# Third attention: two heads' logits as 64-row products on the two halves of the array

## The chip, the cores and the metric

One NeuronCore of one Trainium2 chip runs the whole program. The metric is the device time of one execution in microseconds (us); here the median of three runs.

## The reference, cut to what matters

Two transformer blocks in float32 over 512 tokens of width 1024. The third of its three attentions, the one that changes, has 16 query heads on 4 key heads of width 64, all keys visible:

```python
q = apply_rope_2(rmsnorm(q.reshape(B, T, N_HEADS, HEAD_DIM), q_g), cos, sin)
k = apply_rope_2(rmsnorm(k.reshape(B, T, N_KV_HEADS, HEAD_DIM), k_g), cos, sin)
def one_block(q_blk):
    s = jnp.einsum('bqkgd,bskd->bkgqs', q_blk, k).astype(jnp.float32) * scale
    p = jax.nn.softmax(s, axis=-1).astype(v.dtype)
    return jnp.einsum('bkgqs,bskd->bqkgd', p, v)
```

## The kernel before

Activations lie with features on the 128 partitions and tokens along the free dimension. Every float32 operand of a matmul is split into a high part (rounded to `float32r`) and a low part (the rest), and a product becomes high x high + high x low + low x high (`mul3`).

The program isn't issued as it is written. `Sched.record` notes every operation with its operands; `Sched.order` then simulates the five engines with the prices of `Sched.cost` and emits each engine's queue in the order so found: at each free moment the operation that was recorded first among those ready, unless `later` moved it back. `gate` adds a predecessor. A tile is given a buffer at its first write, in the order of recording, so a missing buffer stops the operations that write to it. PSUM has eight banks: each of the tags `mm`, `lg`, `tp`, `po` has one for itself, four are shared, and `bank` limits what a tag may hold at once.

Layer c is the third attention. For each of its eight pairs of heads, `layer_c` projects q (`fm`, tag `mm`), applies `rope`, and calls `stacks`: tile `a` holds the high part of head 0 on rows 0 to 63 and its low part on rows 64 to 127, tile `b` the same of head 1 the other way round. `doubles` has prepared each key head as `kdh` (high part on both halves) and `kdl` (low part on both halves). So a head's logits for 128 queries are two matmuls over all 128 rows and 512 key columns: stack x `kdh` and stack x `kdl`. `heads` then works head by head: `softmax` makes the logits of four query blocks in `lg` banks, DVE masks them into `pr` with the row's minimum in `mn` (one custom instruction), ACT takes the exponential in place; `turned` transposes `pr` on PE into a `tp` bank and splits it into `th` and `tl`; two products per key block with `v` gather in a `po` bank. `pr` has three buffers, a head needs one. A reciprocal of the row sums follows for both heads together (`late`), then the split into `o`, from which `attn_out` computes the output projection, tile `st` in the profile.

All instructions carry line 423 of the profile, the emitting line; tiles tell them apart.

Of the kernel before, what the change touches and what calls it, by code (L numbers as in the profile page):

```python
# [11 lines left out]
F32 = mybir.dt.float32  # L12
F32R = mybir.dt.float32r
AF = mybir.ActivationFunctionType
ALU = mybir.AluOpType
# [3 lines left out]
P = 128  # L19
S = 512  # L20
# [3 lines left out]
NB = S // P  # L24
# [4 lines left out]
LARGE = 3.0e38  # L29
# [126 lines left out]
class Sched:  # L156
# [92 lines left out]
    @staticmethod  # L249
    def cost(o, outs, ins):  # L250

        ps = any(x.tile.pool.space is not None for x in ins)
        if o.name == "dma_start":
            x = (outs + ins)[0]
            late = 1550 + (x.box[1] - x.box[0]) * x.size * 4 / 360

            return (600, late + 2000) if o.eng == "gpsimd" else (60, late)
        n = max(x.size for x in outs + ins) if o.name in ("tensor_reduce", "bn_stats", "bn_aggr", "max") else outs[0].size
        if o.eng == "tensor":
            x = outs[0].size  # L260
            if o.name == "matmul" and ins[0].tile.dt == F32:
                return max(64, 4 * 0.42 * x), 200
            return max(107 if o.name == "transpose" else 54, 0.417 * x + 2.5), 200
        if o.eng == "scalar":
            aps = sum(isinstance(o.kw.get(k), View) for k in ("bias", "scale", "accum_out"))
            return (51 if ps else 93) + 0.834 * n + 93 * max(0, aps - 1) + (60 if aps == 1 else 0), 130
        if o.eng == "gpsimd":
            if o.name == "tensor_scalar":
                return 160 if n < 16 else 244 + 0.834 * n, 130
            if o.name == "memset":  # L270
                return 100, 130
            return (300 + 164 * n if n < 16 else 100 + 2.2 * n), 130
        c = 68 + 1.042 * n
        if o.name == "scalar_tensor_tensor" and isinstance(o.args[2], View):
            c += 61
        if o.name == "tensor_scalar" and not ps:
            c = 130 + 0.52 * n
        if o.name == "reciprocal":
            c = 70 + 6.3 * n
        return c, 130  # L280
# [219 lines left out]
class Net:  # L500
# [19 lines left out]
        return self.sched.tile(pool, tag, shape, dt, bufs, self.name(tag))  # L520

    def bank(self, tag):
        return self.t(self.pp, tag, [P, S], F32, {"mm": 3, "lg": 3, "tp": 3, "po": 2}[tag])

    def mm(self):
        return self.bank("mm")
# [240 lines left out]
    def softmax(self, pool, npr, lhs, rhs, W, masks, rows, sums, h, late):  # L767
# [20 lines left out]
                nc.gpsimd.tensor_scalar(p, p, rs, 1.0, ALU.mult, ALU.mult)  # L788
        return pr

    def inverses(self, pool, sums, n):

        nc = self.nc
        m = 2 * n
        rs = self.t(pool, "rs", [P, m])
        nc.vector.reciprocal(rs, sums)
        wide = self.t(pool, "top", [P, m * HD], bufs=1)
        nc.scalar.activation(wide.rearrange("p (a d) -> p a d", a=m), rs.rearrange("p (a o) -> p a o", o=1).to_broadcast([P, m, HD]), AF.Copy)
        ps = self.po()
        for b in range(n):  # L800
            nc.tensor.transpose(ps[:, b * P : (b + 1) * P], wide[:, b * P : (b + 1) * P], self.ident)
        return ps[:, : n * P]
# [16 lines left out]
        self.split(th[:, c], tl[:, c], tp[:, c])  # L819
        return th, tl, c  # L820

    def heads(self, pool, npr, nth, lhs, rhs, v, o, masks=None, causal=True, rows=(None, None), blocks=range(NB), narrow=False, late=False):


        nc = self.nc
        n = len(blocks) * P
        W = {i: (i + 1) * P if causal else S for i in blocks}
        keys = range(max(W.values()) // P)
        sums = self.t(pool, "sums", [P, 2 * len(blocks)])
        both = self.t(pool, "o", [P, n], bufs=1)  # L830
        for h in range(2):
            pr = self.softmax(pool, npr, lhs[h], rhs[h], W, masks, rows[h], sums, h, late)
            po = self.po()
            for b in keys:
                th, tl, c = self.turned(pool, nth, pr, W, b)
                if narrow:
                    for x, (part, y) in enumerate(((0, th), (0, tl), (64, th))):
                        nc.tensor.matmul(po[0:64, c], v[h][b][:, part : part + 64], y[:, c], start=b == 0 and x == 0, stop=b == keys[-1] and x == 2)
                else:
                    nc.tensor.matmul(po[:, c], v[h][b], th[:, c], start=b == 0, stop=False)  # L840
                    nc.tensor.matmul(po[:, c], v[h][b], tl[:, c], start=False, stop=b == keys[-1])
            r = slice(64 * h, 64 * h + 64)
            if narrow:
                nc.scalar.activation(both[r], po[0:64, :n], AF.Copy)
            else:
                top = self.t(pool, "top", [P, n], bufs=1)[0:64]
                nc.scalar.activation(top, po[0:64, :n], AF.Copy)
                nc.vector.tensor_tensor(both[r], po[64:128, :n], top, ALU.add)
        if late:
            nc.vector.tensor_tensor(both, self.inverses(pool, sums, len(blocks)), both, ALU.mult)  # L850
        self.split(o[0][:, :n], o[1][:, :n], both)
# [223 lines left out]
    def layer_c(self, x, gate, norm):  # L1075
        nc, I, tc = self.nc, self.I, self.tc
# [7 lines left out]
        with ExitStack() as c1:  # L1084
            pool = c1.enter_context(tc.tile_pool(name="c", bufs=2))
            tab = {}
            for w, col in (("q", V_QG), ("k", V_KG)):
                for m in range(2):
                    a = self.t(pool, f"tab{w}{m}", [P, S], bufs=1)
# [3 lines left out]
            v = [self.t(pool, f"v{b}", [P, 4, P], F32R, 1) for b in range(NB)]  # L1093
            bd = self.t(pool, "bd", [P, 2], bufs=1)
            zero = self.t(pool, "zero", [P, S], bufs=1)
# [5 lines left out]
            def inverse(ps, st):  # L1101

                sq = self.t(pool, "sqh", [P, S], bufs=1)
                nc.scalar.activation(sq, ps, AF.Square)
                for b in range(NB):
                    nc.tensor.matmul(st[:, 2 * b : 2 * b + 2], sq[:, b * P : (b + 1) * P], bd, start=True, stop=True)
                ms = self.t(pool, "msh", [P, 8])
                nc.vector.tensor_scalar(ms, st[:, 0:8], 1.0 / HD, EPS, ALU.mult, ALU.add)
                rr = self.t(pool, "rh", [P, 8], bufs=4)
                nc.gpsimd.tensor_tensor(rr, ms, self.mhalf, ALU.pow)  # L1110
                return rr
# [5 lines left out]
            kd = []  # L1117
            self.tm(I["w_v_c"], xh, xl, evac_v, ("po", "po", "lg", "tp"))
            for ps in kps:
                s = self.rope(pool, ps, tab["k", 0], tab["k", 1], nc.gpsimd)  # L1120
                st = self.lg()
                rr = inverse(ps, st)
# [6 lines left out]
            qs, o = [], []  # L1129
            for j in range(KD + 2):  # L1130
                if j < KD:
                    with self.sched.later(200 if j > 1 else 0):
                        self.low = nc.gpsimd if j > 2 else None
                        ps = q0 if j == 0 else self.fm(I["w_q_c"][j], xh, xl)
                        self.low = None
                        s = self.rope(pool, ps, tab["q", 0], tab["q", 1], nc.gpsimd if j else nc.vector)
                        rr = inverse(ps, ps)
                        qs.append((self.stacks(pool, "st", s, 16), rr))
                if j < 2:
                    continue  # L1140
                j -= 2
                st, rr = qs[j]
                n = j // 2
                o.append(self.two(pool, "st", 16))
                self.heads(pool, 3, 2, [(q, q) for q in st], [kd[n]] * 2, [[x[:, n, :] for x in v]] * 2, o[j], [zero] * NB, causal=False, late=True,
                           rows=[[rr[:, 2 * b + h : 2 * b + h + 1] for b in range(NB)] for h in range(2)])
            self.attn_out(o, I["w_o_c"], gate, norm)

# [314 lines left out]
```

## Time and profile before

| what | value |
|---|---|
| median of three runs | 2582.64 us (2580.6 to 2584.27) |
| profiled execution | 2581.65 us |
| its span, first to last instruction | 2579.8 us |
| PE busy | 2532.9 us, 98% |
| DVE busy | 1584.0 us, 61% |
| ACT busy | 1167.4 us, 45% |
| mean granted TensorE clock | 0.997 |

Busy times are shares of the whole span. PE is the matmul engine, PEld its weight loads, which run beside it; matmuls overlap in a pipeline, so the distance between two starts is the price of one, not its duration. DVE is the vector engine, ACT the scalar engine.

### The profile page before, as it was taken

The page shows a single profiled execution, that of the slowest core. Times are in us where ns is not written, and L with a number is a line of the kernel's source. Part 1 is how long each engine was busy: PE and PEld are TensorE (multiplying, and loading weights), DVE is VectorE, ACT ScalarE, POOL GpSimd, SP SyncE. Part 2 cuts the span into 40 slices and gives each one's busy share as a digit, 9 for nine tenths or more (in the row PEclk, how much of TensorE's full clock was granted, in tenths as well). Part 3 has the DMA queues.
Part 4 walks back from the last instruction along what each step waited for, and adds up shares of the span by engine and source line. Part 5 has one row for each costly group of instructions (what it writes and reads, how often), then busy time and mean ns, then how long its engine had stood idle before and what let it go on. Part 6 is the DMA issues. An engine that isn't in the chain of part 4 may idle for free.

```text
span 2579.8 us, 33446 instructions
## 1 busy us (share of the span) xinstructions
PE 2532.9 (98%) x12614; PEld 2124.3 (82%) x12614; DVE 1584.0 (61%) x2629; ACT 1167.4 (45%) x2104; POOL 404.3 (16%) x453
## 2 busy tenths in 40 slices
PE   8989999999999999999999999999999999999999
PEld 6779888888888888888877988888888888888887
DVE  7998666665488666666797534445447554634443
ACT  5677432334498422334786422333325444523322
POOL 4740100010162000013430200002002110200000
PEclk9999999999999999999999999999999999999999
DMA  4222655543222456542211233322333332333322
GB/s 154 86 70 83 198 188 169 189 139 108 90 72 93 142 186 189 166 159 94 83 37 44 92 98 98 99 93 96 106 106 115 99 95 86 97 98 98 98 97 91
DMA packets 90418, 290.47 MB, mean 113 GB/s; under 512 B 12400, under 2 KB 15728, under 8 KB 90256
## 3 DMA queue, kind: packets, MB, share of 16 engines
q1 hardware_dynamic: 75408, 237.80, 28.7%
q0 software_dynamic: 14848, 50.54, 6.5%
q8 instruction: 99, 1.62, 0.3%
q14 instruction: 63, 0.52, 0.1%
HBM read 277.28 MB, written 2.10 MB: 108 GB/s over the span
## 4 chain that ended last, share of the span: by engine, by line
PE 88%; DVE 7%; ACT 3%; issue 1%; DMA 1%; POOL 0%; SPq 0%; DVEq 0%; ACTq 0%; POOLq 0%
PE mm L423 76%; PE lg L423 4%; PE tp L423 4%; PE po L423 4%; DVE mask L423 1%; DVE st L423 1%; DVE acc L423 1%; DVE xl L423 0%; DVE pr L423 0%; ACT wh L423 0%; DVE o L423 0%; DVE y L423 0%; DVE m L423 0%; DVE wl L423 0%; ACT st L423 0%
## 5 line engine op out<-in xcount | busy, mean ns | idle before, releaser
L423 ACT ACTIVATE wh<-wr 128x1024 fp32r<-128x1024 f32 (+2 forms) x472 | 446.6, 952 | 1092.8 <-PE mm L423 946.0
L423 DVE TENSOR_TENSOR wl<-wr,wh 128x1024 fp32r<-128x1024 f32 (+1 forms) x374 | 449.5, 1202 | 307.6 <-ACT wh L423 298.8
L423 PE MATMUL mm<-xh,wh 128*128 128x512 f32 (+1 forms) x1640 | 625.2, 382 | 8.4 <-ACT wh L423 8.3
L423 PE MATMUL mm<-xl,wh 128*128 128x512 f32 (+1 forms) x1640 | 624.8, 381 | 0.6 <-POOL xl L423 0.4
L423 PE MATMUL mm<-xh,wl 128*128 128x512 f32 (+1 forms) x1640 | 624.9, 381 | 0.0
L423 PE MATMUL mm<-al,wh 128*128 128x512 f32 (+1 forms) x1072 | 407.1, 380 | 0.0
L423 PE MATMUL mm<-ah,wh 128*128 128x512 f32 (+1 forms) x1072 | 407.0, 380 | 0.0
L423 PE MATMUL mm<-ah,wl 128*128 128x512 f32 (+1 forms) x1072 | 406.8, 379 | 0.0
L423 PEld LDWEIGHTS mm<-xh,wh 128*128 128x128 f32 x1640 | 311.4, 190 | 62.6 <-ACT wh L423 9.0
L423 PEld LDWEIGHTS mm<-xl,wh 128*128 128x128 f32 x1640 | 311.9, 190 | 55.6 <-POOL xl L423 1.3
L423 PEld LDWEIGHTS mm<-xh,wl 128*128 128x128 f32 x1640 | 311.7, 190 | 55.0 <-DVE wl L423 0.8
L423 DVE SCALAR_TENSOR_TENSOR h<-mm,mod,h 128x512 f32<-128x512 f32 (+1 forms) x113 | 79.9, 707 | 261.5 <-PE mm L423 261.3
L423 PEld LDWEIGHTS mm<-al,wh 128*128 128x128 f32 x1072 | 201.6, 188 | 38.1
L423 PEld LDWEIGHTS mm<-ah,wh 128*128 128x128 f32 x1072 | 201.6, 188 | 38.1
L423 PEld LDWEIGHTS mm<-ah,wl 128*128 128x128 f32 x1072 | 201.6, 188 | 37.9
L423 POOL TENSOR_TENSOR wl<-wr,wh 128x512 fp32r<-128x512 f32 x98 | 133.1, 1369 | 219.5 <-ACT wh L423 214.7
L423 DVE TENSOR_TENSOR h<-mm,h 128x512 f32<-128x512 f32 (+1 forms) x91 | 56.5, 625 | 140.3 <-PE mm L423 140.3
L423 POOL DMA_DIRECT2D adaw<-in_ada_w x96 | 51.1, 533 | 532.6 <-DVE ada L423 469.5
L423 ACT ACTIVATE pr<-pr,mn 128x128 f32<-128x128 f32 (+2 forms) x192 | 116.6, 610 | 21.9 <-DVE mn L423 21.1
L423 ACT ACTIVATE ah<-a 128x512 fp32r<-128x512 f32 x128 | 81.0, 633 | 83.8 <-DVE a L423 81.7
L423 DVE SCALAR_TENSOR_TENSOR ada<-adaw,cs,ada 128x512 f32<-128x512 f32 x168 | 118.2, 745 | 0.0
L423 DVE TENSOR_TENSOR al<-a,ah 128x512 fp32r<-128x512 f32 x128 | 88.4, 692 | 42.0 <-ACT ah L423 41.9
(260 smaller groups left out, 3848.1 us busy)
## 6 DMA issues: line engine op xcount, KB each, us to landing
adaw<-in_ada_w POOLq DMA_DIRECT2D x96, 512.0 KB, 4.3
wr<-in_w_up SPq DMA_DIRECT2D x64, 512.0 KB
wr<-in_w_down SPq DMA_DIRECT2D x64, 512.0 KB
wr<-in_w_in SPq DMA_DIRECT2D x64, 512.0 KB
wr<-in_w_out SPq DMA_DIRECT2D x64, 512.0 KB
wr<-in_w_gu SPq DMA_DIRECT2D x24, 512.0 KB
wr<-in_w_gv SPq DMA_DIRECT2D x24, 512.0 KB
wr<-in_w_go SPq DMA_DIRECT2D x32, 384.0 KB
```

The costliest lines, as they stand in the source:

```text
L423: getattr(getattr(self.nc, o.eng), o.name)(*args, **kw)
```

## The change

For the third attention alone, a pair's q is only split into a high and a low tile of 128 rows (head 0 on rows 0 to 63, head 1 on rows 64 to 127). `pairs` computes the logits of both heads together: for each of high x high, high x low and low x high one matmul of 64 rows for head 0 and one for head 1, into two banks; all but the first of a group are gated on the second head's first. `softmaxes` masks and exponentiates both heads' blocks in turn, and `heads` transposes and multiplies them afterwards. `lg` may hold four banks in place of three, in the whole program. The planner prices a 64-row `float32r` matmul at half of its former price, at least 108 ns.

```diff
--- before.py
+++ after.py
@@ -260,7 +260,8 @@
             x = outs[0].size
             if o.name == "matmul" and ins[0].tile.dt == F32:
                 return max(64, 4 * 0.42 * x), 200
-            return max(107 if o.name == "transpose" else 54, 0.417 * x + 2.5), 200
+            c = max(107 if o.name == "transpose" else 54, 0.417 * x + 2.5)
+            return (max(108, c / 2) if ins[0].tile.dt == F32R and ins[0].box[1] - ins[0].box[0] == 64 else c), 200
         if o.eng == "scalar":
             aps = sum(isinstance(o.kw.get(k), View) for k in ("bias", "scale", "accum_out"))
             return (51 if ps else 93) + 0.834 * n + 93 * max(0, aps - 1) + (60 if aps == 1 else 0), 130
@@ -520,7 +521,7 @@
         return self.sched.tile(pool, tag, shape, dt, bufs, self.name(tag))
 
     def bank(self, tag):
-        return self.t(self.pp, tag, [P, S], F32, {"mm": 3, "lg": 3, "tp": 3, "po": 2}[tag])
+        return self.t(self.pp, tag, [P, S], F32, {"mm": 3, "lg": 4, "tp": 3, "po": 2}[tag])
 
     def mm(self):
         return self.bank("mm")
@@ -788,6 +789,35 @@
                 nc.gpsimd.tensor_scalar(p, p, rs, 1.0, ALU.mult, ALU.mult)
         return pr
 
+    def pairs(self, outs, q, k, tb, L):
+
+        nc, sched = self.nc, self.sched
+        n = len(sched.ops)
+        for j, (a, b) in enumerate(((q[0], k[0]), (q[0], k[1]), (q[1], k[0]))):
+            for h, ps in enumerate(outs):
+                r = slice(64 * h, 64 * h + 64)
+
+                sched.gate = n + 1 if j else None
+                nc.tensor.matmul(ps[:, :L], a[r, tb], b[r, :L], start=j == 0, stop=j == 2)
+        sched.gate = None
+
+    def softmaxes(self, pool, npr, q, k, W, masks, rows, sums):
+
+        nc = self.nc
+        prs = [self.t(pool, "pr", [P, sum(W.values())], bufs=npr) for _ in range(2)]
+        mns = [self.t(pool, "mn", [P, NB], bufs=4) for _ in range(2)]
+        f = 0
+        for n, (i, L) in enumerate(W.items()):
+            banks = [self.lg() for _ in range(2)]
+            self.pairs(banks, q, k, slice(i * P, (i + 1) * P), L)
+            x = slice(i, i + 1)
+            for h, (ps, pr, mn) in enumerate(zip(banks, prs, mns)):
+                p = pr[:, f : f + L]
+                nc.vector.tensor_tensor_reduce(p, ps[:, :L], masks[i][:, :L], 1.0 if rows[h] is None else rows[h][i], LARGE, ALU.add, ALU.min, mn[:, x])
+                nc.scalar.activation(p, p, AF.Exp, bias=mn[:, x], scale=-1.0, accum_out=sums[:, 2 * n + h : 2 * n + h + 1])
+            f += L
+        return prs
+
     def inverses(self, pool, sums, n):
 
         nc = self.nc
@@ -819,7 +849,8 @@
         self.split(th[:, c], tl[:, c], tp[:, c])
         return th, tl, c
 
-    def heads(self, pool, npr, nth, lhs, rhs, v, o, masks=None, causal=True, rows=(None, None), blocks=range(NB), narrow=False, late=False):
+    def heads(self, pool, npr, nth, lhs, rhs, v, o, masks=None, causal=True, rows=(None, None), blocks=range(NB), narrow=False, late=False, paired=None):
+
 
 
         nc = self.nc
@@ -828,8 +859,10 @@
         keys = range(max(W.values()) // P)
         sums = self.t(pool, "sums", [P, 2 * len(blocks)])
         both = self.t(pool, "o", [P, n], bufs=1)
+        if paired:
+            prs = self.softmaxes(pool, npr, *paired, W, masks, rows, sums)
         for h in range(2):
-            pr = self.softmax(pool, npr, lhs[h], rhs[h], W, masks, rows[h], sums, h, late)
+            pr = prs[h] if paired else self.softmax(pool, npr, lhs[h], rhs[h], W, masks, rows[h], sums, h, late)
             po = self.po()
             for b in keys:
                 th, tl, c = self.turned(pool, nth, pr, W, b)
@@ -1135,14 +1168,16 @@
                         self.low = None
                         s = self.rope(pool, ps, tab["q", 0], tab["q", 1], nc.gpsimd if j else nc.vector)
                         rr = inverse(ps, ps)
-                        qs.append((self.stacks(pool, "st", s, 16), rr))
+                        st = self.two(pool, "st", 16)
+                        self.split(*st, s)
+                        qs.append((st, rr))
                 if j < 2:
                     continue
                 j -= 2
                 st, rr = qs[j]
                 n = j // 2
                 o.append(self.two(pool, "st", 16))
-                self.heads(pool, 3, 2, [(q, q) for q in st], [kd[n]] * 2, [[x[:, n, :] for x in v]] * 2, o[j], [zero] * NB, causal=False, late=True,
+                self.heads(pool, 3, 2, None, None, [[x[:, n, :] for x in v]] * 2, o[j], [zero] * NB, causal=False, late=True, paired=(st, kd[n]),
                            rows=[[rr[:, 2 * b + h : 2 * b + h + 1] for b in range(NB)] for h in range(2)])
             self.attn_out(o, I["w_o_c"], gate, norm)
```

## Rows read from the trace of the kernel before

**Rows 1.** The page's head and first part: busy us, share of the span, instructions.
```profile
span 2579.8 us, 33446 instructions
PE 2532.9 (98%) x12614; PEld 2124.3 (82%) x12614; DVE 1584.0 (61%) x2629; ACT 1167.4 (45%) x2104; POOL 404.3 (16%) x453
```

**Rows 2.** The page's chain that ended last, by line.
```profile
PE mm L423 76%; PE lg L423 4%; PE tp L423 4%; PE po L423 4%; DVE mask L423 1%; DVE st L423 1%; DVE acc L423 1%; DVE xl L423 0%; DVE pr L423 0%; ACT wh L423 0%; DVE o L423 0%; DVE y L423 0%; DVE m L423 0%; DVE wl L423 0%; ACT st L423 0%
```

**Rows 3.** Windows of the third attention: length, engines' busy us, granted clock, DMA.
```profile
core 0: us, PE busy (x) PEld busy (x) DVE busy (x) ACT busy (x) POOL busy (x), PEclk, DMA share, GB/s
1253.40:1405.10 151.70, 147.38 (x797) 116.41 (x795) 133.94 (x273) 124.32 (x270) 39.56 (x28) 1.00 0.14 40
1270.00:1390.00 120.00, 118.82 (x649) 94.10 (x649) 111.75 (x228) 100.08 (x221) 34.89 (x25) 1.00 0.15 45
1404.00:1408.00 4.00, 2.87 (x9) 2.17 (x10) 2.12 (x4) 2.17 (x3) 0.00 (x0) 0.77 0.00 0
```

**Rows 4.** The chain that ended last from 1253.4 to 1405.1 us, by line.
```profile
by line: PE mm L423 28.0%; PE po L423 21.7%; PE tp L423 16.5%; PE lg L423 14.6%; DVE pr L423 3.8%; issue 3.0%; DVE o L423 2.7%; ACT kdh L423 1.7%; ACT pr L423 1.5%; DVE st L423 1.4%; ACT kdl L423 1.2%; ACT top L423 1.2%; ACT th L423 0.6%; D
```

**Rows 5.** Timeline of PE: start us, us, line, operation, count.
```profile
1290.66 0.39 PE L423 MATMUL lg<-kdh,st 128*128 128x512 f32 x1
...
1291.12 0.39 PE L423 MATMUL lg<-kdl,st 128*128 128x512 f32 x1
...
1300.93 0.39 PE L423 MATMUL lg<-kdl,st 128*128 128x512 f32 x1
1301.16 0.40 PE L423 MATMUL mm<-xl,wh 128*128 128x512 f32 x1
...
1302.66 0.60 PE L423 MATMUL tp<-ident,pr 128*128 128x128 f32 x4
1303.01 0.48 PE L423 MATMUL lg<-kdh,st 128*128 128x512 f32 x1
1303.32 0.40 PE L423 MATMUL lg<-kdl,st 128*128 128x512 f32 x1
```

**Rows 6.** Groups by form, 1253.4 to 1405.1 us: busy us, mean ns, idle before.
```profile
L423 DVE CUSTOM_DVE_ANT_0 pr<-lg,zero,rh 128x512 f32<-128x512 f32 x64 | 46.3, 743 | 2.1 <-PE lg L423 1.7
...
L423 PE MATMUL lg<-kdl,st 128*128 128x512 f32 x64 | 25.7, 407 | 0.0
...
L423 DVE TENSOR_TENSOR st<-q,st 64x512 fp32r<-64x512 f32 x14 | 9.6, 686 | 2.4 <-ACT st L423 1.9
...
L423 ACT ACTIVATE st<-q 64x512 fp32r<-64x512 f32 x14 | 8.7, 625 | 2.8 <-POOL q L423 2.6
...
L423 DVE TENSOR_TENSOR st<-o,st 128x512 fp32r<-128x512 f32 x7 | 4.8, 689 | 0.1
```

**Rows 7.** Timeline of weight loads in a stretch of 256-column products.
```profile
1225.88 0.19 PEld L423 LDWEIGHTS mm<-xh,wl 128*128 128x128 f32 x1
...
1226.00 0.19 PEld L423 LDWEIGHTS mm<-xh,wh 128*128 128x128 f32 x1
```

**Rows 8.** The `lg` tile, whole span: idle before its instructions, us and times.
```profile
  DVE mn L423: 2.8, 10
```

**Rows 9.** Timeline of PE at the stage's end.
```profile
1405.13 1.29 PE L423 MATMUL mm<-st,wh 128*128 128x512 f32 x4 [1.45 <-ACT st L423]
1406.22 0.63 PE L423 MATMUL mm<-st,wl 128*128 128x512 f32 x1
1406.65 0.63 PE L423 MATMUL mm<-st,wh 128*128 128x512 f32 x1
```

**Rows 10.** Timeline of PE and PEld around the eight-row transposes.
```profile
24.50 0.27 PE L423 MATMUL po<-ident,r 128*128 128x128 f32 x1
...
24.70 0.13 PEld L423 LDWEIGHTS po<-ident,rl 8*128 8x128 f32 x1 [0.17 <-issue]
24.71 0.22 PE L423 MATMUL po<-ident,rl 8*128 8x8 f32 x1
...
25.45 0.22 PE L423 MATMUL po<-ident,rl 8*128 8x8 f32 x1 [0.39 <-DVE wi L423]
...
25.60 0.50 PE L423 MATMUL mm<-xh,wh 128*128 128x512 f32 x1
...
25.93 0.39 PE L423 MATMUL mm<-xl,wh 128*128 128x512 f32 x1
```

## The prediction

> **What bounds the kernel now.** I read the page's engine totals first [rows 1]: PE is busy 98% of the span. The chain that ended last, by line, spends only 4% on the logits banks (`lg`), and that 4% belongs to three attentions and two other stages together [rows 2]. So the change can move only a small share, and the question is what sets the time where the third attention runs.
>
> Its scores are masked by 64 DVE instructions of their own form, between 1254 and 1393 us by the view of the score tile; from there the first and last matmuls of the stage gave me the stretch 1253.4 to 1405.1 us, 151.70 us. In it PE is busy 147.38 us, DVE 133.94, ACT 124.32 [rows 3]. PE's busy time is a modelled sum, so I ask the chain for the same stretch [rows 4]: `mm` 28.0%, `po` 21.7, `tp` 16.5 and `lg` 14.6 are PE, 80.8% together; some 14% is single waits for DVE and ACT. The reader is to see that PE is the limit here, that its holes are filled with projections (`mm`), and that DVE stands close behind: from 1270 to 1390 us it is busy 111.75 of 120 us, 93% [rows 3]. A shorter PE queue is worth something here, but not microsecond for microsecond.
>
> PE's prices are distances from start to start [rows 5]: a 512-column matmul behind another 0.23 us (1300.93 to 1301.16); a 128-column transpose 0.11 us (four take 0.60 us, one alone 0.27 [rows 10], so three steps 0.33); a long matmul right behind transposes holds the next one off for 0.31 us and not 0.23 (1303.01 to 1303.32), since its weight load wasn't hidden.
>
> **What the change removes and adds.** *Logits.* There are 8 pairs of heads x 4 query blocks = 32 groups; the 64 low products of today are in [rows 6], as many high ones stand beside them. A group now has 2 heads x 2 products of 128 rows, 4 x 0.23 = 0.92 us. Afterwards it has 3 products x 2 heads, each on 64 rows, six instructions of 512 columns. No row of this trace shows two matmuls side by side in the array, so the price is bounded. Full overlap of the halves: 3 x 0.23 = 0.69 us, 0.23 less per group, 7.4 us in all. No overlap: 6 x 0.23 = 1.38 us, 0.46 more, 14.7 us in all. Weight loads allow the first: one takes 0.19 us, but in a stretch of 256-column products they start 0.12 us apart [rows 7], so two fit into 0.24 us. The halves share neither rows, banks nor a semaphore, so I take overlap as likelier; but if the second head's load starts 0.12 us late, a group ends 0.12 us later (0.81 us). I take the middle of the overlapped case, 0.75 us: 32 x 0.17 = -5.4 us.
>
> The Trainium skill ("TensorE: Matmul & The Clock Gate", Part 3, packing small matmuls) says that matmuls in distinct row groups run concurrently and gives 3.07x for four of 32 rows. No run here shows it; by its ideal form the sum would be the -7.4 us end.
>
> *Cut groups.* The emitted order puts urgent transposes and `po` products between logits: of the 20 pairs of logit products between 1268.7 and 1306.4 us I find one cut, the one whose halves start at 1290.66 and 1291.12 [rows 5]. Six instructions leave more places for it, and a product left alone loses its overlap, 0.12 us. At an estimated 0.4 cuts per group: 32 x 0.4 x 0.12 = +1.5 us.
>
> *Stacks.* For each pair `stacks` issued two 64-row instructions on ACT and two on DVE, 0.63 and 0.69 us each; the split issues one of 128 rows on each, and the split of `o` shows that rows don't change the price (0.69) [rows 6]. For the 7 pairs in the stretch DVE loses 7 x 0.69 = 4.8 us and ACT 7 x 0.63 = 4.4 us. I cost it at nothing: PE's work covers it. If PE stops being the limit it is worth up to 4.8 us.
>
> *Order of the softmaxes.* Both heads of a pair are now masked and exponentiated before the first is transposed, with three `pr` buffers as before. While head 0 of pair j is turned, head 1 of pair j+1 has no `pr`; its logits wait written in their banks, and behind them, through the banks, later logits, transposes and `mm` products. Below this costs nothing, since DVE has 7% free and gets 4.8 us; above it is a rival. The chain is 80% PE today, so I count 80% of what PE saves: (-5.4 + 1.5) x 0.8 = -3.1 us.
>
> *Fourth logits bank.* It holds for every stage that uses `lg`. In the whole trace PE's queue sat idle before logits for 2.8 us until `mn`, the masking's last instruction, had freed a bank or a value [rows 8]; that bounds the gain. Against it, a bank that logits hold is missing for `mm`, `tp` or `po`, which I bound by the same 2.8 us. I take 0. The planner's new price (108 ns for each 64-row product) changes only the order; it fits only if the halves overlap, and where they don't, each group is planned 0.7 us too short.
>
> *Tail.* At the end PE waits 1.45 us for `st`, and then the granted clock is 0.77 over four microseconds, partly the lower level of 1.2 GHz: matmuls come 0.43 us apart and not 0.23 [rows 3, 9]. The same chain of copy, add, inverse and split still ends the stage; I cost it at 0, with 2 us either way.
>
> **Sum.** -3.1 us. The profiled execution took 2581.65 us for a span of 2579.8 [rows 1]; 1.85 us lie around it. So 2578.5 us for such an execution; the median of the runs, 2582.64, is 1.0 us above it: 2579.5.
>
> **The rivals.**
> (1) *Changing between 128 and 64 rows stops PE.* Every group changes twice, 64 times in all. The only change of rows in this trace is at the eight-row transposes [rows 10]: behind a transpose of 128 rows at 24.50 us the first of eight rows starts 0.21 us later where 0.11 is usual, and its load sat idle 0.17 us for nothing that the profile shows. On the way back the long matmul comes 0.15 us after the last short one, and the next only 0.33 us behind it. That is 0.05 to 0.10 us for a change and up to 0.10 for the unhidden load: 0.15 to 0.35 us per group, 4.8 to 11.2 us. On top of -3.1: +1.7 to +8.1, middle +4.9, 2587 us. It turns the sign from 0.05 us per change (3.1/64). Against it: one place, and eight rows, not 64.
> The Trainium skill ("TensorEngine Tiling (Array Packing)", Key Properties) speaks for this rival and against the change: a change of tiling mode drains the engine. The idle load of [rows 10] agrees with it; no row has 64 rows.
> (2) *No overlap.* +14.7 us less about 1 that cuts no longer cost: 2596 us. For it: all matmuls of the trace start one after another. Against it: nothing orders work on different rows and banks.
> (3) *DVE takes over.* For it: 93% busy. A pair takes (1393 - 1254)/8 = 17.4 us. If the coarse hand-over of `pr` holds each pair for more than 4 x 0.17 = 0.7 us, PE's saving is gone; at twice that the time is 2582 to 2587 us. Against it: DVE's masking waited only 1.7 us for logits in the whole stretch [rows 6], so work is there when it is free.
> (4) *Full overlap, nothing lost.* -7.4 us, and perhaps 2 more from banks and the freed DVE: 2573 to 2575 us.
>
> **How the numbers follow.** A measurement of this kernel can't tell less than 0.2%, about 5.2 us, from no change: faster ends at 2577.5, slower begins at 2587.8. Forecast (own range 2575 to 2583): 0.37. (4): 0.20. (1): 0.18. (2): 0.14. (3): 0.11. Faster: all of (4) and a third of the forecast, 0.32. Slower: all of (2), half of (1), a fifth of (3), and 0.03 from disorder in other stages: 0.28. Same: the rest, 0.40. The range leaves out most of (2) and the best of (4): 2571 to 2594.
>
> **What would show it.** In the changed profile the stage holds 192 logit matmuls of 64 rows. Right: starts in couples of some 0.01 to 0.12 us, six in about 0.75 us, the stage near 148 us, DVE above 90% from 1270 to 1390. Rival 1: a hole of 0.1 us or more ahead of the first 64-row load and ahead of the 128-row load behind the group. Rival 2: six starts 0.23 us apart. Rival 3: logits written long before their mask, PE idle for DVE or ACT. Wrong altogether if other stages with `lg` move by more than 3 us because of the fourth bank.

## The result and the profile after

The changed kernel takes 2602.98 us, the median of four runs (2602.16 to 2604.73); beside them the kernel before took 2581.69. The ratio is 1.0082, interval 1.0064 to 1.0099: 21.3 us slower. The forecast of 2579.5 is wrong, and so is its range, which ended at 2594. Of the runs 7 and 9 below, one execution in eleven each took 5100 us (in the trace of that of run 7 most 512-column products stand 0.44 us apart); the ratios leave it out, and the medians move by less than 0.5 us without it.

The page's head and engine totals, to be held against [rows 1]:

```profile
span 2603.0 us, 33541 instructions
PE 2556.5 (98%) x12678; PEld 2125.1 (82%) x12678; DVE 1580.3 (61%) x2621; ACT 1168.0 (45%) x2096; POOL 407.7 (16%) x453
```

The share of PE hides the loss: 98% both times. Its busy time is up by 23.6 us and the span by 23.2. To compare the third attention I cut both traces at the same two instructions: ahead of the last four transposes of the stage before it (1250.67 us before, 1253.24 after), and ahead of the projection product that waits for `st` at its end (1405.13 [rows 9] and 1430.11). These instructions in PE's timelines, before and after:

```profile
1250.67 0.60 PE L423 MATMUL lg<-ident,o 128*128 128x128 f32 x4
```

```profile
1253.24 0.60 PE L424 MATMUL lg<-ident,o 128*128 128x128 f32 x4
...
1430.11 1.23 PE L424 MATMUL mm<-st,wh 128*128 128x512 f32 x4 [1.44 <-ACT st L424]
```

The first window is of the kernel before; the others are of the changed kernel: the stage, 4 us within it, and 4 us behind it (us, busy time and count of each engine, granted clock, DMA):

```profile
1250.60:1405.10 154.50, 150.18 (x812) 118.75 (x810) 136.00 (x275) 127.04 (x275) 41.41 (x30) 1.00 0.14 40
```

```profile
core 0: us, PE busy (x) PEld busy (x) DVE busy (x) ACT busy (x) POOL busy (x), PEclk, DMA share, GB/s
1253.20:1430.10 176.90, 173.90 (x875) 118.05 (x873) 131.70 (x269) 124.63 (x268) 44.50 (x30) 0.99 0.12 35
1368.00:1372.00 4.00, 4.00 (x19) 2.97 (x19) 1.90 (x8) 4.00 (x10) 2.90 (x2) 0.57 0.01 4
1430.00:1434.00 4.00, 3.67 (x13) 2.13 (x13) 3.08 (x5) 2.68 (x5) 0.00 (x0) 1.00 0.00 0
```

176.90 us where there were 154.50: 22.4 of the 23.2 us are here. The stage begins 2.6 us later than before, and what follows it is 1.8 us shorter: behind it the granted clock is 1.00, where [rows 3] have 0.77. Of its own loss 1.7 us is one dip of the granted clock at 1368 to 1372 us (0.57). PE is listed as idle for 3.0 us of it, where it had 4.3. DVE lost 4.3 us of work and ACT 2.4 (forecast: 4.8 and 4.4), and nothing came of it. The chain of that stretch, before and after:

```profile
by line: PE mm L423 27.5%; PE po L423 21.3%; PE tp L423 16.2%; PE lg L423 14.4%; DVE pr L423 3.7%; ACT kdh L423 3.2%; issue 3.0%; DVE o L423 2.6%; ACT pr L423 1.5%; DVE st L423 1.3%; ACT kdl L423 1.2%; ACT top L423 1.2%; ACT th L423 0.6%; D
```

```profile
by line: PE mm L424 29.3%; PE lg L424 24.6%; PE po L424 20.7%; PE tp L424 16.4%; POOL q L424 1.3%; issue 1.2%; ACT top L424 1.0%; DVE st L424 1.0%; DVE o L424 0.8%; DVE q L424 0.8%; DVE h L424 0.8%; ACT st L424 0.7%; DVE tl L424 0.7%; DVE p
```

Times length, `lg` goes from 22.2 to 43.5 us. But `mm` rose too (42.5 to 51.8), `tp` by 4.0 and `po` by 3.7, though the change touches none of them: PE's four together from 122.7 to 161.0 us, 38.3 more, while all else on the chain fell from 31.8 to 15.9. So 16 of PE's 38 us took the place of time that the chain had spent on other engines and their waits.

What the `mm` and `po` products lost is in the waits of the stretch (who waited, for whom; us in total, times, the longest). "issue" means that nothing the profile shows was missing. Before, that stretch has one such wait of PEld, of 0.3 us:

```profile
PEld lg L424 <- issue: 12.6, 52, 0.4
PEld mm L424 <- issue: 10.9, 37, 0.4
...
PEld po L424 <- issue: 4.1, 16, 0.4
PEld tp L424 <- issue: 3.0, 10, 0.4
```

And the timeline of PE and PEld shows where they stand: start, us, operation, count, idle time before:

```profile
1292.51 0.50 PE L424 MATMUL lg<-kdh,st 64*128 64x512 f32 x2 [0.19 <-DVE st L424]
1292.94 0.19 PEld L424 LDWEIGHTS mm<-xh,wl 128*128 128x128 f32 x1 [0.25 <-issue]
1292.94 0.50 PE L424 MATMUL mm<-xh,wl 128*128 128x512 f32 x1
...
1293.98 0.40 PE L424 MATMUL mm<-xh,wl 128*128 128x512 f32 x1
1294.31 0.18 PEld L424 LDWEIGHTS lg<-kdh,st 64*128 64x128 f32 x1 [0.37 <-issue]
1294.31 0.50 PE L424 MATMUL lg<-kdh,st 64*128 64x512 f32 x1
1294.31 0.29 PEld L424 LDWEIGHTS lg<-kdl,st 64*128 64x128 f32 x2
1294.32 0.73 PE L424 MATMUL lg<-kdl,st 64*128 64x512 f32 x2
...
1294.66 0.39 PE L424 MATMUL lg<-kdh,st 64*128 64x512 f32 x1
1294.98 0.14 PEld L424 LDWEIGHTS tp<-ident,pr 128*128 128x128 f32 x1 [0.37 <-issue]
```

Two things are to be seen. The overlap is real: at 1294.31 and 1294.32 two products begin 0.01 us apart. And each change of rows costs: the first product of 64 rows starts 0.33 us behind the last of 128 where [rows 5] have 0.23, the next couple 0.35 us behind the first, and the transpose at 1294.98 0.32 us behind the last logit. Ahead of both changes of rows PEld is idle for 0.37 us. The group is torn, too: its first couple stands alone at 1292.51, the other four products at 1294.31, with five others between.

A run of 64-row products without one of 128 rows between is a *stretch* below. Counted in the queue that PE is given, the 192 products form 73 stretches, not 32, and 34 of these hold a single product. Counting each overlapped couple and each lone product as one slot of 0.23 us, they take 126 slots; before there were 128, and whole groups would need 96.

### The profile page after: what moved, and what is told of

Read it like the earlier page. It is cut to its first block, busy times and chain, and to the rows that moved or that the text cites. A ratio compares the mean times of both kernels' runs of the same rounds, so it can differ in the third digit from the quotient of the medians.

```text
span 2603.0 us, 33541 instructions
## 1 busy us (share of the span) xinstructions
PE 2556.5 (98%) x12678; PEld 2125.1 (82%) x12678; DVE 1580.3 (61%) x2621; ACT 1168.0 (45%) x2096; POOL 407.7 (16%) x453
## 4 chain that ended last, share of the span: by engine, by line
PE 88%; DVE 7%; ACT 2%; issue 1%; DMA 1%; POOL 0%; SPq 0%; DVEq 0%; ACTq 0%; POOLq 0%
PE mm L424 75%; PE lg L424 5%; PE tp L424 4%; PE po L424 4%; DVE mask L424 1%; DVE st L424 1%; DVE acc L424 1%; DVE m L424 1%; DVE y L424 0%; DVE xl L424 0%; ACT pr L424 0%; ACT wh L424 0%; DVE o L424 0%; ACT st L424 0%; DVE pr L424 0%
## 5 line engine op out<-in xcount | busy, mean ns | idle before, releaser
L424 ACT ACTIVATE pr<-pr,mn 128x128 f32<-128x128 f32 (+2 forms) x192 | 116.4, 609 | 21.3 <-DVE mn L424 20.3
L424 DVE TENSOR_TENSOR tl<-tp,th 128x512 fp32r<-128x512 f32 (+1 forms) x224 | 104.7, 495 | 20.5 <-ACT th L424 11.9
```

The source lines that it names most:

```text
L424: getattr(getattr(self.nc, o.eng), o.name)(*args, **kw)
```

## The experiments

The theories, as the expectations name them. **S**: every change between 128 and 64 rows stops PE, so the number of stretches sets the loss. **N**: the halves don't overlap enough, so the number of products sets it. **O**: the new order of the softmaxes, or the fourth `lg` bank that starves other tags, sets it. The kernel before took 2581.36 us beside the runs 1 to 4, 2582.06 beside 5 to 8, 2582.59 beside 9 to 11 (medians). The 0.27 us that S takes for a stretch is about the changed kernel's own loss over its 73 stretches (20/73). Of each edit only the lines that carry it are shown.

**1. The fourth bank alone**, in the kernel before:

```diff
-        return self.t(self.pp, tag, [P, S], F32, {"mm": 3, "lg": 3, "tp": 3, "po": 2}[tag])
+        return self.t(self.pp, tag, [P, S], F32, {"mm": 3, "lg": 4, "tp": 3, "po": 2}[tag])
```

> The kernel before with a fourth logits bank and nothing else. Theory S (each change between 128 and 64 rows stops PE; the emitted order has 73 stretches of 64-row products): the bank is a side matter, about +2 us, as the first logits of the changed kernel came 2.6 us later than before. Theory O (the new order of the softmaxes and the fourth bank cost the time by starving other tiles): +10 us or more here or in the next run.

2585.82 us, ratio 1.0014 (1.0004 to 1.0023). A small loss, a fifth of what is to be explained. It is not all the bank's: these executions had a lower mean clock, and at equal mean clock some 1 to 3 us are left.

**2. The new order alone**: masks and exponentials of both heads ahead of the transposes, four banks, the planner's new price, but stacks and two products of 128 rows per head as before.

```diff
+    def pairs(self, outs, q, k, tb, L):
+        for h, ps in enumerate(outs):
+            for j in range(2):
+                nc.tensor.matmul(ps[:, :L], q[h][:, tb], k[j][:, :L], start=j == 0, stop=j == 1)
```

> The changed kernel's order (both heads masked and exponentiated before the first is transposed, four logits banks), but each head's logits as two 128-row products of the stacks, as before. S: within 4 us of before, 2580 to 2586. O: most of the loss is here, 2595 or more.

2582.28 us, 0.9997 (0.9986 to 1.0009). O falls: the order and the `pr` buffers cost nothing that can be measured, and with them the fourth bank does no harm either.

**3. Changes of rows without the change.** The kernel before; in layer c each head's second product reads only the 64 rows of the high part of q. It leaves out low x low; number, order and columns of the products stay.

```diff
+                if j and pool.name == "c":
+                    r = slice(64 * h, 64 * h + 64)
+                    self.sched.ops[-1].args = (ps[:, :L], a[r, tb], b[r, :L])
```

> The kernel before, instruction for instruction, but each head's second product reads only the 64 rows with the high part (it leaves out low x low). As many matmuls and columns as before, 62 stretches of 64 rows, nothing that could overlap. S: 62 x 0.27 us = +17 us, about 2598. N (the loss is the number of products, six for four, since halves do not overlap; changing rows costs nothing): no change, 2582. O: no change.

2599.27 us, 1.0062 (1.0047 to 1.0077): 17.9 us for 62 stretches of a single product, 0.29 us each. Nothing but the rows of 64 products differs, all at a granted clock of 1.00 in the stage. Its timeline:

```profile
1300.78 0.47 PE L423 MATMUL lg<-kdh,st 128*128 128x512 f32 x1
1301.18 0.18 PEld L423 LDWEIGHTS lg<-kdl,st 64*128 64x128 f32 x1 [0.24 <-issue]
1301.18 0.50 PE L423 MATMUL lg<-kdl,st 64*128 64x512 f32 x1
1301.61 0.19 PEld L423 LDWEIGHTS lg<-kdh,st 128*128 128x128 f32 x1 [0.24 <-issue]
1301.61 0.49 PE L423 MATMUL lg<-kdh,st 128*128 128x512 f32 x1
...
1302.04 0.50 PE L423 MATMUL lg<-kdl,st 64*128 64x512 f32 x1
1302.46 0.19 PEld L423 LDWEIGHTS mm<-xl,wh 128*128 128x128 f32 x1 [0.25 <-issue]
```

Starts are 0.40 to 0.43 us apart where 0.23 is usual: 0.2 us per change, both ways, and the load isn't made ahead. PE's queue holds the same instructions in the same order as before. The Trainium skill ("TensorEngine Tiling (Array Packing)", Key Properties) says that a change of tiling mode drains the engine; this trace agrees, with those 0.24 us of idle load.

**4 and 5. The changed kernel's very order, with other rows.** From the second pair of heads on, the six products of a group read all 128 rows (4), or both heads read rows 0 to 63 (5). In 4 the logits mix both heads; in 5 head 1's logits are head 0's. Only the operands change after planning (for 5: `a[0:64, tb], b[0:64, :L]`):

```diff
                 nc.tensor.matmul(ps[:, :L], a[r, tb], b[r, :L], start=j == 0, stop=j == 2)
+                if self.later_pair:
+                    sched.ops[-1].args = (ps[:, :L], a[:, tb], b[:, :L])
```

> The changed kernel in its very order, but from the second pair of heads on the six products of a group read all 128 rows (the logits are then sums over both heads, wrong). No changes of rows there, no overlap possible. S: 7/8 of 64 more matmuls of 0.23 us than before and some 6 stretches left: +13 +2 +2 us, about 2598, faster than the changed kernel although nothing overlaps. N: the same as the changed kernel, 2603, within 1 us. O: 2603 too.

> The changed kernel in its very order, but from the second pair of heads on both heads' products read rows 0 to 63 (head 1's logits are then those of head 0, wrong). The same 73 stretches of 64 rows, nothing that can overlap. S: the changed kernel's stretches hold 126 slots of 0.23 us where its 192 products would need 192 one by one; without overlap 7/8 of 66 slots more, +13 us on 2603: 2616. N: no change from the changed kernel, 2603.

4: 2590.99 us, 1.0032 (1.0020 to 1.0044), 7 us under what S had expected. 5: 2620.43 us, 1.0146 (1.0128 to 1.0164). Between before and after lie three steps: 56 more products of 128 rows in this order and six stretches of the first pair of heads, +9.6 us (56 x 0.23 = 12.9 on PE, and the six stretches); the same products on 64 rows without overlap, +29.4; overlap of the halves, -17.4. The timeline of 5 shows that products on the same half don't overlap: three starts from 1291.19 to 1291.66 us, 0.23 us each.

```profile
1290.61 0.74 PE L424 MATMUL lg<-kdh,st 64*128 64x512 f32 x2
1291.19 0.63 PE L424 MATMUL lg<-kdl,st 64*128 64x512 f32 x2
1291.66 0.39 PE L424 MATMUL lg<-kdh,st 64*128 64x512 f32 x1
```

Opposite halves do overlap, so N falls, and the changes of rows are the largest term. Run 5 carries a disturbance of its own. Windows of its stage:

```profile
1320.00:1324.00 4.00, 4.00 (x24) 2.81 (x22) 3.94 (x8) 3.87 (x9) 4.00 (x3) 1.00 0.03 6
1324.00:1328.00 4.00, 4.00 (x9) 1.79 (x8) 1.97 (x6) 1.45 (x3) 2.25 (x3) 0.56 0.38 131
1328.00:1332.00 4.00, 4.00 (x14) 2.94 (x14) 1.57 (x4) 0.83 (x2) 0.84 (x1) 0.50 0.00 0
1332.00:1336.00 4.00, 4.00 (x9) 1.95 (x8) 2.58 (x5) 2.40 (x7) 0.00 (x0) 0.66 0.00 0
```

In this execution (2623.34 us) the granted clock falls to the level of 1.2 GHz for some ten microseconds, and once more at 1376 to 1388 us: 8.5 us lost by (1 - clock) x length. Two of the four executions had a mean clock of 0.992 (2623.3 and 2623.6 us), two of 0.995 (2617.1 and 2617.5). So I compare at 0.995, where run 4 took 2593.0 us and the changed kernel 2603.6 on average: the changes are then 24 us for 67 stretches, 0.36 us each, and the overlap gives back 14, close to the 13 that S expected.

**6 and 7. Welded groups.** The changed kernel, but the first product of a group takes both heads' banks at once, and the rest of the group goes ahead of everything: six products can't be torn (6), or, with two query blocks and four banks at once, twelve (7). For this the planner sets two (7: four) of the banks aside for the logits of the stage.

```diff
+        sched.ops[n].mates = [outs[1].tile]
+        for o in sched.ops[n + 1 :]:
+            o.prio -= 10000
```

> The changed kernel, with each group of six welded: its first product waits until both heads' banks are free, the other five go ahead of all else. 35 stretches and 102 slots in the emitted order, where the changed kernel has 73 and 126. S: 26 slots fewer than before's 128 = -6.0 us, 35 x 0.27 = +9.5, the fourth bank about +2: 2587, 16 us faster than the changed kernel. N: 2603.

> As the welded one, but two query blocks at once, four banks and twelve products in a stretch: 18 stretches, 100 slots. S: -6.4 + 18 x 0.27 = -1.6 us, the fourth bank +2, and whatever it costs that four banks must be free at once: 2582 to 2586. If the fewer stretches bring nothing over the welded one, the price hangs on something other than their number.

6: 2584.84 us, 1.0014 (1.0004 to 1.0023), 35 stretches and 102 slots. 7: 2581.45 us, 0.9995 (0.9986 to 1.0005), 18 stretches and 100 slots. The same 192 products: with fewer changes of rows, and some 25 slots fewer since couples stay whole, the loss goes from 21 us to 3 and to none, and no gain is left. The timeline of 6 shows what a whole group costs:

```profile
1299.82 0.40 PE L442 MATMUL po<-th,v 128*128 128x512 f32 x1
1300.15 0.19 PEld L442 LDWEIGHTS lg<-kdh,st 64*128 64x128 f32 x2 [0.37 <-issue]
1300.15 0.50 PE L442 MATMUL lg<-kdh,st 64*128 64x512 f32 x2
...
1300.48 0.40 PE L442 MATMUL lg<-kdl,st 64*128 64x512 f32 x2
...
1300.71 0.40 PE L442 MATMUL lg<-kdh,st 64*128 64x512 f32 x2
1301.04 0.19 PEld L442 LDWEIGHTS po<-tl,v 128*128 128x128 f32 x1 [0.36 <-issue]
1301.04 0.50 PE L442 MATMUL po<-tl,v 128*128 128x512 f32 x1
...
1301.38 0.60 PE L442 MATMUL tp<-ident,pr 128*128 128x128 f32 x4
```

From start to start 0.33, 0.33, 0.23, 0.33, 0.34 us. In step they would be 0.23 each: the entry costs 0.10, the second couple, whose load wasn't hidden, 0.10, the exit 0.10, and the product behind it 0.11. A stretch costs PE 0.41 us and saves 0.23 per group.

**8. Three banks** in the changed kernel (run 1's edit the other way round).

> The changed kernel with three logits banks as before. 68 stretches and 123 slots in the emitted order. S: 5 x 0.27 + 3 x 0.23 = 2 us and some 3 us for the bank itself (what it cost the kernel before): 2598. O, as far as it rests on banks: worse than the changed kernel, since a pair needs two banks at a time: 2605 or more.

2599.25 us, 1.0060 (1.0043 to 1.0077): 68 stretches, 123 slots. That is 3.7 us less than the changed kernel, and five stretches fewer explain the better half of it (below). The fourth bank isn't the cause.

**9, 10 and 11. Runs 7, 6 and 2 with the fourth bank in layer c alone**, three elsewhere as before:

```diff
+            if q is p.slots.get("lg") and q["used"] > 2 and not self.wide.start <= q["next"] < self.wide.stop:
+                return False
```

> The welded kernel of twelve products, with the fourth logits bank in the third attention only. With the bank everywhere the median was 2581.45, 0.6 below the kernel before. S: at 18 stretches the switches (18 x 0.27 = 4.9 us) nearly eat the 28 saved slots (6.4 us): 2578 to 2582, faster than before by 0 to 0.15%. If the bank costs time in the other attentions, this gains up to 3 us more: 2576 to 2579.

> The welded kernel of six products, with the fourth bank in the third attention only. S: the same 35 stretches, 3 us behind the one of twelve: 2582 to 2586. If the fourth bank elsewhere was its loss, 2581.

> The new order of the softmaxes with 128-row stacks and the fourth bank in the third attention only. With the bank everywhere it was level with before (2582.3). S has nothing to change here: 2580 to 2583. If the bank elsewhere costs 2 to 3 us, 2579.

9: 2582.33 us, 0.9995 (0.9986 to 1.0004). 10: 2586.01, 1.0018 (1.0009 to 1.0027). 11: 2581.43, 0.9997 (0.9988 to 1.0007). None differs from its twin: what four banks do to other stages is nothing that can be measured. The twelve of run 9, and the window and chain of its stage:

```profile
1301.15 0.19 PEld L444 LDWEIGHTS lg<-kdh,st 64*128 64x128 f32 x2 [0.17 <-issue]
1301.15 0.51 PE L444 MATMUL lg<-kdh,st 64*128 64x512 f32 x2
...
1301.48 0.40 PE L444 MATMUL lg<-kdl,st 64*128 64x512 f32 x2
...
1301.71 0.63 PE L444 MATMUL lg<-kdh,st 64*128 64x512 f32 x4
...
1302.17 0.39 PE L444 MATMUL lg<-kdl,st 64*128 64x512 f32 x2
...
1302.40 0.40 PE L444 MATMUL lg<-kdh,st 64*128 64x512 f32 x2
1302.73 0.19 PEld L444 LDWEIGHTS mm<-xh,wl 128*128 128x128 f32 x1 [0.36 <-issue]
```

```profile
1256.30:1410.00 153.70, 146.98 (x866) 113.92 (x867) 131.85 (x267) 119.93 (x262) 42.18 (x27) 1.00 0.12 35
```

```profile
by line: PE mm L444 21.5%; PE po L444 18.0%; PE tp L444 11.9%; PE lg L444 10.3%; ACT pr L444 6.3%; DVE tl L444 4.2%; DVE pr L444 4.0%; DVE q L444 3.5%; issue 3.2%; DVE h L444 2.8%; DVE o L444 2.7%; DVE wl L444 2.1%; DMA rot<-q 2.0%; ACT top
```

Twelve products in 1.58 us up to the next one of 128 rows, where two groups of four take 8 x 0.23 = 1.84 [rows 5]; the entry ahead of them and one more unhidden load behind the exit add 0.2 us. So even here nearly all of the saving is spent, and with PE at 62% of the chain its remainder would hardly show.

One price now gives all kernels, on PE: 0.41 us per stretch, and 0.23 us per slot more or less than 128.

| kernel | stretches | slots | PE, worked out | measured (median) |
|---|---|---|---|---|
| after | 73 | 126 | 29.93 - 0.46 = +29.5 us | +21.3 us |
| 3, one product each | 62 | 128 | +25.4 | +17.9 |
| 8, three banks | 68 | 123 | 27.9 - 1.2 = +26.7 | +17.2 |
| 6, six welded | 35 | 102 | 14.4 - 6.0 = +8.4 | +2.8 |
| 7, twelve welded | 18 | 100 | 7.4 - 6.4 = +0.9 | -0.6 |

The signs of all but the last, which can't be told from no change, come out, and of a large loss on PE 64 to 72% is felt (63% of the 15.3 us of run 4 with its six stretches, 88% of the 27.5 us that run 5's 67 add); the rest takes the place of waits that were there before, as the chain of after showed. The smaller share at 6 was not taken further apart.

## Why the prediction was wrong

**The step that failed** is the price of a group, "32 x 0.17 = -5.4 us". It rested on two things. That the halves overlap was right. That entering and leaving 64 rows is free was wrong: rival 1 had the mechanism, the place in the trace [rows 10] and the sign, and got 0.18. Its price, 0.15 to 0.35 us per group, was too low on PE, which loses 0.41 us per stretch, and near in the time, 0.29 us in run 3. (Its parts, two changes of 0.05 to 0.10 and a load of up to 0.10, add up to 0.10 to 0.30.) What it had not was the number of changes.

**The number of changes.** Rival 1 counted 32 groups and 64 changes. The queue has 73 stretches and 146 changes. The term "cut groups" had seen that groups are torn and put it at 0.4 cuts per group; it is 41 cuts for 32 groups, 1.3, and each cut costs not "its overlap, 0.12 us" but another stretch. It took the whole saving as well: 126 slots instead of 96. The estimate was made from a queue in which each pair of logits needs one bank; now five of six products hang on the second head's bank (its own first product, and the four that are gated on that one), and transposes, `po` and `mm` products that are ready go between. With 73 stretches at 0.29 us and no saving left, rival 1 would have given 21 us, about 2603.

**The other terms.** *Stacks*: right, and the 4.3 us of DVE's freed time had no effect, since PE became still more the limit. *Order of the softmaxes* at nothing: right (run 2), so rival 3 was wrong. *Fourth bank* at 0, bound 2.8 us: alone it costs 4.5 us by its median (interval 1.0 to 5.9), some of it clock (below), so that the bound may hold. *80% of PE's time is felt*: 63 to 88% in the runs. *Tail*: it was not the half-clock end of [rows 9]; after shows 1.00 there, and has a dip of 0.57 at 1368 us instead. Rival 2 gave 2596 for a false reason. The sign to look for, "a hole of 0.1 us or more ahead of the first 64-row load and ahead of the 128-row load behind the group", was the right one: 52 holes ahead of `lg` loads, 63 ahead of the others.

**What stays open.** Why the load behind a change of rows comes so late (0.33 us behind the start of the product before it, 1293.98 and 1294.31 above) is not shown by a trace; that it does, is. The loss in run 6, a third of what PE's prices give, is open as well.

## What to carry to other kernels

Packing small products into the array pays by the stretch, not by the product: each entry and exit cost 0.2 us here, so that a stretch between 128-row work needs, as an estimate from 0.41 us per stretch and 0.23 us per group, about two groups of six 512-column products to break even. Before costing such a change count, in the queue that the scheduler will emit, how often the row count changes; a price per group is worth nothing while others may step in between. And a "free" side effect in the trace (an idle load with no cause shown) is a price to be multiplied, even where it occurs once.

## What the runs showed of the hardware

Two `float32r` products of 64 rows on opposite halves start 0.01 us apart and go on at 0.23 us per couple, the price of one; on the same half they start 0.23 us apart, one by one. The Trainium skill ("TensorE: Matmul & The Clock Gate", Part 3, packing small matmuls) says that matmuls on distinct tiles of the array run beside each other; the trace agrees, with the 0.01 us. Loads of 128 rows behind 512-column products of 128 rows are hidden (0.19 us within 0.23); where the row count changes, the load sits idle 0.17 to 0.37 us.

The granted clock fell while PE was listed as busy without a gap: in run 5 the 16 us from 1320 to 1336 are busy 4.00 of 4.00 in each window, at 1.00, 0.56, 0.50 and 0.66.

Much of the spread between executions of one kernel goes with the mean granted clock. In 67 executions of the kernel before, those at 0.994, 0.996 and 0.998 took 2587.0, 2582.2 and 2579.2 us on average, 2 us per thousandth. The changed kernel's four were at 0.995 and 0.996; against executions of the kernel before at the same value it is 19 to 20 us slower (2603.6 to 2584.5, 2602.2 to 2582.2). So one to two of its 21.3 us are clock, and the rest is the lengthening of the stage: 22.4 us in the profiled execution, 20.7 without the dip of the clock in it.
